# In-projection order: the chunk of latent keys and values ahead of the two chunks of rotary queries and keys

## The chip, the cores and the metric

The kernel runs on one core of one Trainium2 chip. A core has five engines that each work through their own list of instructions in order: PE (TensorE, matrix products), DVE (VectorE), ACT (ScalarE), POOL (GpSimd) and SP (SyncE, which here issues the DMAs). [...] The metric is the device time of one launch in microseconds (us). The median of three runs of the kernel before is 3787.1 us (3786.85 to 3792.39).

## The reference

Two layers of a transformer-like trunk are applied to 128 context tokens and 1024 latent tokens, 1152 tokens of width 1024 in all. One layer begins with one product, the in-projection, whose columns are split into the inputs of three mixers:

```python
z = jnp.einsum('bsd,dn->bsn', h, P['w_in'][l])
hq, hff, hfb, hi, hg, mq, mkv, mkr, gq, gk, gv = jnp.split(z, IN_OFFSETS, axis=-1)
hg_out, s_f, s_b = _hgrn_mixer(hq, hff, hfb, hi, hg, lb, s0f, s0b, P['hg_norm'][l])
ckv = _rms(mkv, P['mla_kv_norm'][l])
gq = _rms(gq.reshape(...), P['gqa_q_norm'][l]);  gk = _rms(gk.reshape(...), P['gqa_k_norm'][l])
gq = _rope_2d(gq, row, col);  ak = concat([gk_c, _rope_2d(gk, row, col)])
```

The HGRN mixer is a gated linear recurrence over the tokens in both directions. The MLA mixer is attention over compressed keys and values (mq, mkv, mkr). The GQA mixer is attention with six query heads and two key heads, normalised per head and rotated in two dimensions (gq, gk, gv). The three outputs go through an output projection and a layer norm, then a SwiGLU feed-forward block and a second layer norm follow.

## The kernel before

The tokens are nine tiles of 128. A layer is four phases: the in-projection with the HGRN recurrence (phase_b), both attentions (phase_c), the output projection (phase_d) and the feed-forward block (phase_e). Products are made exact by splitting each operand into a high and a low part and adding three products (mm3, lines 110 to 112).

In phase_b a *chunk* of the in-projection is 256 columns (288 for chunk "b") for all nine tiles: token_chunk (L355) loads the chunk's weights, and for each tile runs 24 matmuls into a PSUM bank and then evacuates it. The evacuations differ, and they matter here:

- chunk 3 (output gate of HGRN), ev_raw: one ACT copy, one store to DRAM.
- chunks 5 and 6 (rotary queries and keys; called q0 and q1 below), ev_q (L403): ACT squares and copies, DVE sums (L412), POOL forms the reciprocal root in two instructions (L118, L119), DVE scales by it (L415) and by the norm's row (L417, once per tile for q0, twice for q1), POOL rotates (L397 twice, L400, L401), and the tile is stored to the DRAM tensor zq.
- chunk "b" (latent keys and values, values of GQA, rotary part of the MLA key), ev_k (L437): ACT squares and copies, the same two POOL instructions on one column, one DVE instruction (L445), and the rotation on 32 columns only; stored to zk.
- chunk 7 (MLA queries, called mq below), ev_m (L427): ACT squares, the two POOL instructions on one column, one DVE instruction (L434), which frees the PSUM bank.

Beside each tile of mq goes one *turn* of the GQA heads (gqa_turn, L517): it reads zq of one token tile back from DRAM (tile tx), transposes it on PE (L534), copies on ACT (L537, L541), and takes low parts on POOL (L542 and a L104). It needs both q0 and q1 of that tile in DRAM. hgrn_gate (L717) takes the gate chunk through a sigmoid and two POOL products (L726, L728). The first attention group of phase_c needs all ten turns.

hgrn (L572) walks the nine tiles with seven levels and a diagonal each. A level is: DVE forms differences (L641, L644 twice), ACT takes the exponential (L646), POOL makes two products (L648, L650), PE multiplies (L655), DVE writes under a mask (L660). The last L650 of a layer is the last POOL instruction of the recurrence.

The program is not run in the order in which it is written. A list scheduler replays the recorded instructions and writes a fixed order for each engine, in which the matmuls of the chunks that are written behind hgrn fill the gaps of the recurrence on PE. What was written earlier has precedence. The chunks' PSUM banks are few: two ("a") in layer 0, three ("aad") in layer 1 (L341), and the staging tiles st number three (L368). So PE can run only a few tiles ahead of the evacuations.

Of the kernel before, what the change touches and what calls it, by code (L numbers as in the profile page):

```python
# [53 lines left out]
class Build:  # L54
# [280 lines left out]
    def phase_b(self, l, first=None):  # L335
# [4 lines left out]
        b = "b"  # L340
# [14 lines left out]
        def token_chunk(name, evac):  # L355
            ws = self.w_in(*name)
            n = 288 if name[1] == "b" else 256
            for t in range(NT):
                ps = self.ps("A")
                terms = [(self.hts(t, k, 0), self.hts(t, k, 1), hi[:, k - k0, :], lo[:, k - k0, :])  # L360
                         for k0, k1, hi, lo in ws for k in range(k0, k1)]
                self.mm3(ps[:, :n], terms)
                evac(t, ps)
                if t % 2:
                    self.fill()

        def stage():
            return self.t("b2", [P, 384], tag="st", bufs=3)  # L368

        def ev_raw(name):  # L370
            def ev(t, ps):
                st = stage()
                nc.scalar.copy(st[:, :256], ps[:, :256])
                nc.sync.dma_start(z[name][t], st[:, :256])
            return ev
# [7 lines left out]
        def tables(t):  # L383
            tb = self.t("b2", [P, 192], tag="tb", bufs=2)
            nc.sync.dma_start(tb, A["rope_tok"][:, t - 1, :])
            return tb

        def rope(x, tb, off, heads, half):

            w = 4 * half  # L390
            xv = x.rearrange("p (h a s f) -> p h a s f", h=heads, a=2, s=2)
            cos = tb[:, off:off + w].unsqueeze(1).broadcast_to([P, heads, w])
            sin = tb[:, off + w:off + 2 * w].rearrange("p (a s f) -> p a s f", a=2, s=2)
            t2 = self.tmp()
            tv = t2[:, :heads * w].rearrange("p (h a s f) -> p h a s f", h=heads, a=2, s=2)
            for s in range(2):
                nc.gpsimd.tensor_tensor(tv[:, :, :, s, :], xv[:, :, :, 1 - s, :],  # L397
                                        sin[:, :, s, :].unsqueeze(1).broadcast_to([P, heads, 2, half]), op=ALU.mult)
            xm = x.rearrange("p (h w) -> p h w", h=heads)
            nc.gpsimd.tensor_tensor(xm, xm, cos, op=ALU.mult)  # L400
            nc.gpsimd.tensor_tensor(x, x, t2[:, :heads * w], op=ALU.add)  # L401

        def ev_q(half):  # L403
            def ev(t, ps):
                st = stage()
                x = st[:, :256]
                sq = self.tmp()
                nc.scalar.activation(sq[:, :256], ps[:, :256], AF.Square)
                nc.scalar.copy(x, ps[:, :256])
                ss = self.t("small", [P, 4], tag="ss4", bufs=3)  # L410
                r = self.t("small", [P, 4], tag="r4", bufs=3)
                nc.vector.reduce_sum(ss, sq[:, :256].rearrange("p (h f) -> p h f", h=4), axis=AX.X)  # L412
                self.rsq(r, ss, 1 / 64, 4)
                xv = x.rearrange("p (h f) -> p h f", h=4)
                nc.vector.tensor_tensor(xv, xv, r.unsqueeze(2).broadcast_to([P, 4, 64]), op=ALU.mult)  # L415
                for h0, n, g in (((0, 4, 0),) if half == 0 else ((0, 2, 0), (2, 2, 64))):
                    nc.vector.tensor_tensor(xv[:, h0:h0 + n], xv[:, h0:h0 + n],  # L417
                                            rows[:, g:g + 64].unsqueeze(1).broadcast_to([P, n, 64]), op=ALU.mult)
                if t == 0:
                    if half:  # L420
                        nc.sync.dma_start(A["o_gk"][0, l].rearrange("s h f -> s (h f)"), x[:, 128:256])
                else:
                    rope(x, tables(t), 0, 4, 16)
                nc.sync.dma_start(z["q"][t][:, half * 256:half * 256 + 256], x)
            return ev
# [62 lines left out]
        self.hgrn(l, cst, masks)  # L488

        token_chunk((l, 3), ev_raw("g"))  # L490
        token_chunk((l, 5), ev_q(0))
        token_chunk((l, 6), ev_q(1))

# [8 lines left out]
                self.gqa_turn(l, 1, 1, "G")  # L502
            self.gqa_turn(l, 1, t + (t > 0), "G")

        token_chunk((l, "b"), ev_k)
        token_chunk((l, 7), ev_mq)
        self.hgrn_gate(l)
        self.fill(100)
# [920 lines left out]
```

## Time and profile before

| | |
|---|---|
| median of three runs | 3787.1 us |
| profiled execution | 3788.79 us |
| its span, first to last instruction | 3787.0 us |
| mean granted TensorE clock | 0.981 of full |
| PE busy | 3667.2 us (97% of the span) |
| DVE busy | 2021.7 us (53%) |
| ACT busy | 1380.3 us (36%) |
| POOL busy | 1100.7 us (29%) |
| recurrence with chunks b, q0, q1, mq, layer 0 | about 178 to 492 us |
| the same, layer 1 | about 2080 to 2347 us |

A busy PE is no proof of a full PE, since its matmuls are pipelined and their ends are modelled. The granted clock (PEclk) says more: it falls where PE had waited. POOL and DVE, at 29% and 53% of the whole span, are close to full in the two stretches of the recurrence, which are about 15% of the time.

### The profile page before, as it was taken

Reading aid. Unit: us, or ns where it says so; the run is one execution under the profiler, and the core shown is the slowest. Engines: PE = TensorE matmul, PEld = TensorE weight load, DVE = VectorE, ACT = ScalarE, POOL = GpSimd, SP = SyncE. Lnnn points to the kernel's source line nnn. Section 1 sums busy time; section 2 is a strip of 40 time slices with the busy share of each in tenths; the row PEclk is TensorE's granted clock in tenths of the full one; section 3 lists DMA queues with packets and bytes.
Section 4 is the critical chain, followed back from the end, with each engine's and each line's share of the span. In section 5 each row is a group of like instructions: output and inputs, shape, how many; then the busy total and the mean of one; then the engine's idle time right before and its main releaser. Section 6 shows DMA issues by size and latency. Waiting matters only on the chain.

```text
span 3787.0 us, 60397 instructions
## 1 busy us (share of the span) xinstructions
PE 3667.2 (97%) x23734; PEld 3210.9 (85%) x23734; DVE 2021.7 (53%) x3906; ACT 1380.3 (36%) x3283; POOL 1100.7 (29%) x1394
## 2 busy tenths in 40 slices
PE   8999899999999999999999989999999999999997
PEld 6878777788788888999989878778877999999996
DVE  3489456556564333333366894665567533333336
ACT  3433466666341111111144335666654211111111
POOL 1158850211161000000432786511126600000054
PEclk9998899999999999999999998999999999999998
DMA  6521421001134331111231115100012311111131
GB/s 240 179 64 43 117 65 25 15 7 35 59 130 157 101 106 51 51 40 48 96 128 59 51 44 140 28 20 15 7 55 73 114 41 47 41 40 45 45 95 73
DMA packets 185967, 263.78 MB, mean 70 GB/s; under 512 B 68657, under 2 KB 114353, under 8 KB 185170
## 3 DMA queue, kind: packets, MB, share of 16 engines
q1 hardware_dynamic: 185682, 259.92, 21.7%
q8 instruction: 187, 3.06, 0.3%
q14 instruction: 98, 0.80, 0.1%
HBM read 218.47 MB, written 38.77 MB: 68 GB/s over the span
## 4 chain that ended last, share of the span: by engine, by line
PE 81%; DVE 7%; POOL 4%; ACT 3%; issue 2%; DMA 2%; SPq 0%; POOLq 0%; DVEq 0%; ACTq 0%
PE b L110 10%; PE b L112 10%; PE b L111 10%; PE d L855 7%; PE c L806 5%; PE a L110 5%; PE b L784 5%; PE a L111 4%; PE a L112 4%; PE a L784 3%; PE b L655 2%; PE c L110 2%; PE c L112 2%; PE c L111 2%; PE d L111 2%
## 5 line engine op out<-in xcount | busy, mean ns | idle before, releaser
L111 PE MATMUL b<-h,w 128*128 128x384 f32 x1848 | 622.4, 337 | 3.6 <-DVE h L104 2.7
L110 PE MATMUL b<-h,w 128*128 128x384 f32 x1848 | 623.8, 338 | 0.1
L112 PE MATMUL b<-h,w 128*128 128x384 f32 x1848 | 621.8, 337 | 0.0
L103 ACT CAST w<-raw 128x1024 fp32r<-128x1024 f32 (+2 forms) x192 | 198.7, 1036 | 803.4 <-PE c L111 262.7
L104 DVE TENSOR_TENSOR w<-raw,w 128x1024 fp32r<-128x1024 f32 (+3 forms) x188 | 242.1, 1295 | 367.9 <-ACT w L103 362.4
L110 PEld LDWEIGHTS b<-h,w 128*128 128x128 f32 x1848 | 347.4, 188 | 17.8 <-issue 7.6
L111 PEld LDWEIGHTS b<-h,w 128*128 128x128 f32 x1848 | 347.6, 188 | 10.3 <-DVE h L104 4.5
L112 PEld LDWEIGHTS b<-h,w 128*128 128x128 f32 x1848 | 347.5, 188 | 8.0 <-issue 5.0
L1245 POOL TENSOR_TENSOR acc<-acc,lg 128x512 f32<-128x512 f32 x36 | 49.1, 1378 | 935.4 <-DVE acc L1231 931.7
L110 PE MATMUL a<-w,h 128*128 128x256 f32 (+1 forms) x960 | 287.2, 299 | 8.4 <-DVE st L445 4.9
L855 PE MATMUL d<-pt,v 128*64 128x128 f32 x3456 | 288.9, 285 | 0.4 <-DVE m L856 0.4
L111 PE MATMUL a<-w,h 128*128 128x256 f32 (+1 forms) x960 | 281.0, 293 | 0.0
L112 PE MATMUL a<-w,h 128*128 128x256 f32 (+1 forms) x960 | 279.7, 292 | 0.0
L806 PE MATMUL c<-ident,p 128*128 128x128 f32 x1728 | 272.0, 279 | 6.7 <-ACT p L790 2.9
L855 PEld LDWEIGHTS d<-pt,v 128*64 128x64 f32 x3456 | 186.3, 136 | 76.7 <-issue 61.7
L785 DVE TENSOR_REDUCE m<-b 128x1 f32<-128x384 f32 x346 | 188.5, 554 | 112.8 <-PE b L784 112.1
L806 PEld LDWEIGHTS c<-ident,p 128*128 128x128 f32 x1728 | 200.4, 141 | 47.2 <-issue 16.3
L790 ACT ACTIVATE p<-b,nm 128x384 f32<-128x384 f32 x346 | 198.6, 582 | 72.4 <-DVE nm L788 66.3
L110 PEld LDWEIGHTS a<-w,h 128*128 128x128 f32 x960 | 188.1, 196 | 30.9 <-ACT m L380 6.7
L111 PEld LDWEIGHTS a<-w,h 128*128 128x128 f32 x960 | 188.1, 196 | 5.4 <-issue 1.9
L112 PEld LDWEIGHTS a<-w,h 128*128 128x128 f32 x960 | 187.5, 195 | 4.2 <-issue 1.7
L1202 DVE TENSOR_TENSOR gate<-gate,b 128x384 f32<-128x384 f32 x110 | 60.9, 553 | 242.5 <-PE b L112 242.5
(391 smaller groups left out, 8483.1 us busy)
## 6 DMA issues: line engine op xcount, KB each, us to landing
w<-in_w_ada_dram SPq DMA_DIRECT2D x96, 512.0 KB, 4.4
raw<-in_w_ffn_in_dram SPq DMA_DIRECT2D x88, 512.0 KB, 3.5
raw<-in_w_ffn_out_dram SPq DMA_DIRECT2D x44, 512.0 KB, 3.6
raw<-in_w_in_a_dram SPq DMA_DIRECT2D x32, 512.0 KB, 4.4
xs<-acc SPq DMA_DIRECT2D x36, 256.0 KB, 4.1
u<-xs SPq DMA_DIRECT2D x36, 256.0 KB, 2.5
raw<-in_w_out_dram SPq DMA_DIRECT2D x16, 512.0 KB, 4.3
tx<-zq SPq DMA_DIRECT2D x72, 96.0 KB, 2.4
```

Of the source, the lines that this page charges most:

```text
L103: self.nc.scalar.copy(hi, src)
L104: (eng or self.nc.vector).tensor_tensor(lo, src, hi.bitcast(F32), op=ALU.subtract)
L110: self.nc.tensor.matmul(out, ah, bh, start=i == 0, stop=False)
L111: self.nc.tensor.matmul(out, ah, bl, start=False, stop=False)
L112: self.nc.tensor.matmul(out, al, bh, start=False, stop=i == n - 1)
L655: nc.tensor.matmul(ps[:, j * P:(j + 1) * P], X[r, j, :], Q[r, j, :], start=True, stop=True)
L784: nc.tensor.matmul(ps, a, bfn(c * 384, 384), start=k == 0, stop=k == len(ops) - 1)
L785: nc.vector.reduce_max(mx[:, c:c + 1], ps, axis=AX.X)
L790: nc.scalar.activation(pt[:, c * 384:(c + 1) * 384], tiles[c], AF.Exp, bias=nm, accum_out=sm[:, u, c:c + 1])
L806: nc.tensor.transpose(pt[:, (2 * i + u) * P:(2 * i + u + 1) * P], g["p"][u][:, kt * P:(kt + 1) * P], self.ident)
L855: nc.tensor.matmul(po[h * 64:(h + 1) * 64, :P], g["v"](k, h), turned[s // 2][:, o:o + P], start=k == 0, stop=k == 8)
L1202: nc.vector.tensor_tensor(g, g, ps[:, :384], op=ALU.mult)
```

## The change

One line of phase_b moves: chunk "b" is written in front of q0 and q1 instead of behind them. Nothing else is edited.

```diff
@@ phase_b
         self.hgrn(l, cst, masks)
 
         token_chunk((l, 3), ev_raw("g"))
+        token_chunk((l, "b"), ev_k)
         token_chunk((l, 5), ev_q(0))
         token_chunk((l, 6), ev_q(1))
 
...
-        token_chunk((l, "b"), ev_k)
         token_chunk((l, 7), ev_mq)
```

The same instructions are issued, with the same operands and sizes. Their order in the engines' lists changes in the stretch from the first of these chunks to the first attention group, in both layers; the rest of the lists is the same but for a few neighbours exchanged.

On PE in layer 0, the two rows behind the last products of the recurrence (L682, L679). Before, they and six more tiles are chunk b (128x288):

```order
L682 MATMUL c_3370<-it_3136,at_3140 128x64 x2
L679 MATMUL c_3370<-Sf_1658,m_466 128x128
L682 MATMUL c_3370<-it_3136,at_3140 128x64 x2
L110 MATMUL a_4652<-w_4554,h_71_245 128x288
L111 MATMUL a_4652<-w_4555,h_71_245 128x288
```

In the changed kernel, at the same place:

```order
L682 MATMUL c_3370<-it_3136,at_3140 128x64 x2
L679 MATMUL c_3370<-Sf_1658,m_466 128x128
L682 MATMUL c_3370<-it_3136,at_3140 128x64 x2
L110 MATMUL a_4808<-w_4528,h_74_250 128x256
L111 MATMUL a_4808<-w_4529,h_74_250 128x256
```

Behind the recurrence stand now three tiles of q1 and nine of mq in place of seven of b and nine of mq.

On POOL in layer 0, the rows from the last L650 on. Before (rsv, r with x1: reciprocal roots of b; st 128x32: rotation of b; it: the HGRN gate):

```order
L650 TENSOR_TENSOR Q_3353<-qT_3138,E_3348 128x256
L400 TENSOR_TENSOR st_4524<-st_4524,tb_4537 128x256
L119 TENSOR_TENSOR r_960_4598<-rsv_961_4601,mhalf_76 128x1
L119 TENSOR_TENSOR r_966_4637<-rsv_967_4640,mhalf_76 128x1
L400 TENSOR_TENSOR st_4634<-st_4634,tb_4644 128x32
L726 TENSOR_TENSOR it_5431<-it_5431,u_5433 128x256
L401 TENSOR_TENSOR st_4524<-st_4524,t_4539 128x256
L401 TENSOR_TENSOR st_4634<-st_4634,t_4646 128x32
```

In the changed kernel (rsv, r with x4 and st 128x256: q1):

```order
L650 TENSOR_TENSOR Q_3353<-qT_3138,E_3348 128x256
L728 TENSOR_TENSOR it_5431<-it_5431,hgn_464 128x256
L118 TENSOR_SCALAR rsv_979_4702<-ss_977_4699 128x4
L400 TENSOR_TENSOR st_4649<-st_4649,tb_4662 128x256
L119 TENSOR_TENSOR r_978_4700<-rsv_979_4702,mhalf_76 128x4
L401 TENSOR_TENSOR st_4649<-st_4649,t_4664 128x256
L397 TENSOR_TENSOR t_4710<-st_4695,tb_4708 128x8x16 x2
L400 TENSOR_TENSOR st_4695<-st_4695,tb_4708 128x256
```

Seven tiles of q1 are rotated behind the last L650 now; before, it was the end of one.

On POOL in layer 1 of the changed kernel, the rows up to the first reciprocal root of mq (r_4619; te: a turn's copy, t_23459: rotation of the last q1 tile):

```order
L104 TENSOR_TENSOR K_4608_23471<-te_23837,K_4607_23470 128x128
L726 TENSOR_TENSOR it_23985<-it_23985,u_23987 128x256
L397 TENSOR_TENSOR t_23459<-st_23444,tb_23457 128x8x16 x2
L118 TENSOR_SCALAR rsv_4620_23514<-ss_4618_23511 128x1
L118 TENSOR_SCALAR rsv_4632_23573<-ss_4630_23570 128x1
L118 TENSOR_SCALAR rsv_4641_23623<-ss_4639_23620 128x1
L726 TENSOR_TENSOR it_23992<-it_23992,u_23994 128x256
L728 TENSOR_TENSOR it_23985<-it_23985,hgn_19173 128x256
L400 TENSOR_TENSOR st_23444<-st_23444,tb_23457 128x256
L119 TENSOR_TENSOR r_4619_23512<-rsv_4620_23514,mhalf_76 128x1
```

All nine rotations of q1 but the last instruction of the last one, seven turns, and seven and six of the gate's two products stand ahead of it; before, the first reciprocal root of mq stood behind chunk b's small instructions and ahead of all turns.

## Rows read from the trace of the kernel before

**Rows 1.** Windows, both recurrences and tails: length; busy PE, PEld, DVE, ACT, POOL; clock.

```profile
245.00:417.00 172.00, 155.80 (x1081) 136.23 (x1081) 155.94 (x360) 66.77 (x148) 147.42 (x199) 0.89 0.15 44
417.00:492.00 75.00, 63.09 (x455) 60.94 (x451) 16.76 (x37) 28.47 (x87) 46.07 (x101) 0.91 0.54 148
2105.00:2298.00 193.00, 180.34 (x1258) 158.62 (x1256) 164.47 (x397) 76.01 (x175) 164.03 (x238) 0.91 0.17 52
2298.00:2347.00 49.00, 42.73 (x343) 40.83 (x339) 15.36 (x30) 24.10 (x69) 38.23 (x72) 0.95 0.71 193
```

**Rows 2.** Windows of 20 us: before q0 begins, and in layer 0's tail.

```profile
220.00:240.00 20.00, 20.00 (x141) 16.01 (x139) 15.53 (x37) 7.50 (x15) 7.55 (x9) 1.00 0.26 80
440.00:460.00 20.00, 15.10 (x103) 14.31 (x102) 4.81 (x8) 11.41 (x32) 18.50 (x40) 0.87 0.78 202
```

**Rows 3.** Groups by line, DVE, 245 to 417 us: busy, mean ns, idle before.

```profile
L415 DVE TENSOR_TENSOR st<-st,r 128x256 f32<-128x256 f32 x18 | 13.4, 742 | 3.6 <-POOL r L119 3.6
L417 DVE TENSOR_TENSOR st<-st,rows 128x128 f32<-128x128 f32 x18 | 7.9, 470 | 0.1
L412 DVE TENSOR_REDUCE ss<-t 128x4 f32<-128x256 f32 x18 | 7.4, 409 | 0.3
```

**Rows 4.** Groups by line, DVE, 417 to 492 us.

```profile
L434 DVE SCALAR_TENSOR_TENSOR st<-a,r,rows 128x256 f32<-128x256 f32 x9 | 4.3, 483 | 16.9 <-POOL r L119 16.9
L445 DVE SCALAR_TENSOR_TENSOR st<-a,r,rows 128x128 f32<-128x128 f32 x9 | 3.1, 350 | 26.4 <-POOL r L119 20.6 <-DMA tx<-zq 5.8
```

**Rows 5.** Groups by line, POOL, 245 to 417 us.

```profile
L119 POOL TENSOR_TENSOR r<-rsv,mhalf 128x4 f32<-128x4 f32 x18 | 19.8, 1104 | 0.3
L397 POOL TENSOR_TENSOR t<-st,tb 128x128 f32<-128x128 f32 x32 | 16.0, 516 | 6.1 <-DVE st L417 5.3 <-ACT kT L614 0.8
L401 POOL TENSOR_TENSOR st<-st,t 128x256 f32<-128x256 f32 x15 | 12.8, 850 | 0.2
L118 POOL TENSOR_SCALAR rsv<-ss 128x4 f32<-128x4 f32 x18 | 5.0, 275 | 9.4 <-DVE ss L412 8.5
```

**Rows 6.** Groups by line, POOL, 417 to 492 us.

```profile
L542 POOL TENSOR_TENSOR Q<-te,Q 64x384 fp32r<-64x384 f32 x9 | 9.9, 1102 | 0.7
L119 POOL TENSOR_TENSOR r<-rsv,mhalf 128x1 f32<-128x1 f32 x18 | 9.9, 550 | 0.7
L728 POOL TENSOR_TENSOR it<-it,hgn 128x256 f32<-128x256 f32 x8 | 5.9, 734 | 0.2
L104 POOL TENSOR_TENSOR K<-te,K 128x128 fp32r<-128x128 f32 x10 | 5.3, 530 | 0.7
L118 POOL TENSOR_SCALAR rsv<-ss 128x1 f32<-128x1 f32 x16 | 3.2, 198 | 19.5 <-ACT t L432 13.3 <-ACT t L442 5.4
L401 POOL TENSOR_TENSOR st<-st,t 128x256 f32<-128x256 f32 x1 | 0.7, 727 | 0.0
```

**Rows 7.** Timeline of POOL: start, duration; last L650 and mq's roots, both layers.

```profile
415.66 0.72 POOL L650 TENSOR_TENSOR Q<-qT,E 128x256 f32<-128x256 f32 x1
...
477.82 0.55 POOL L119 TENSOR_TENSOR r<-rsv,mhalf 128x1 f32<-128x1 f32 x1
...
490.61 0.55 POOL L119 TENSOR_TENSOR r<-rsv,mhalf 128x1 f32<-128x1 f32 x1
...
2296.45 0.74 POOL L650 TENSOR_TENSOR Q<-qT,E 128x256 f32<-128x256 f32 x1
...
2344.45 0.55 POOL L119 TENSOR_TENSOR r<-rsv,mhalf 128x1 f32<-128x1 f32 x1
```

**Rows 8.** Timeline of PE: two neighbouring matmuls of an mq tile.

```profile
475.07 0.28 PE L111 MATMUL a<-w,h 128*128 128x256 f32 x1
475.19 0.28 PE L112 MATMUL a<-w,h 128*128 128x256 f32 x1
```

**Rows 9.** Chain of waits by line, 245 to 417 us.

```profile
by line: PE b L655 14.1%; issue 10.6%; DVE E L644 6.8%; PE a L110 6.5%; PE a L111 5.6%; POOL Q L650 5.4%; PE a L112 5.3%; DVE at L660 5.1%; POOL X L648 4.2%; POOL r L119 3.8%; DVE E L641 3.4%; PE c L682 2.4%; DVE st L415 2.3%; DVE st L417 2
```

**Rows 10.** Waits of PE, 417 to 492 us: total, times, longest.

```profile
PE a L110 <- DVE st L434: 2.9, 2, 1.7
```

## The prediction

> **What bounds the kernel now.** I read the windows of the two recurrences first, then the groups by line of POOL and DVE in them, then the timeline of POOL behind them, and the waits of PE last. "Recurrence" is the stretch up to POOL's last L650 of a layer; "tail" is what follows, up to POOL's reciprocal root for the last tile of mq, after which the first attention group can take its banks.
>
> In the recurrences DVE is busy 155.9 of 172 us (91%) and 164.5 of 193 (85%), POOL 147.4 (86%) and 164.0 (85%) [rows 1]. PE is busier by its own count, but its clock averages 0.89 and 0.91 there, so it did wait. The chain of waits passes through PE, DVE and POOL in turn and none holds it alone [rows 9]. The first part is another matter: at 220 to 240 us, before q0, PE is busy 20.00 of 20.00 at full clock [rows 2]. So the recurrence is filled by PE at its beginning, and held by DVE and POOL where q0 and q1 are evacuated.
>
> The tails differ by layer. From the end of the last L650 (415.66 + 0.72 = 416.4) to the end of mq's last root (490.61 + 0.55 = 491.2) layer 0 takes 74.8 us; layer 1 takes from 2297.2 to 2345.0, 47.8 us [rows 7]. POOL has room there: 46.1 busy of 75 and 38.2 of 49; DVE has much (16.8 and 15.4) [rows 1].
>
> **The change part by part.** No instruction is added or removed. Work moves over the last L650.
>
> 1. *Recurrence, DVE.* I count in the order what DVE has done up to its last L641. Layer 0: L412 18 before and 12 now, L415 18 and 11, L417 27 and 13 (all of the missing ones are q1's halves), L445 none and 9. In times [rows 3, 4]: 6 x 0.409 + 7 x 0.742 + 14 x 0.470 - 9 x 0.350 = 11.1 us less. Layer 1: 5, 6 and 12 fewer, 6 more L445: 2.0 + 4.5 + 5.6 - 2.1 = 10.0 us less. If DVE alone set the pace, the last L650 would come 11 and 10 us earlier. If PE did, it would come no earlier. PE gets no relief: in layer 0 seven tiles of b come into the recurrence and three of q1 leave it. A matmul of 256 columns takes 0.12 us [rows 8], so a tile of 24 takes 2.8; with 288 columns I estimate 3.2 from that. 7 x 3.2 - 3 x 2.8 = 14 us more for PE, and PE's unfilled time by its own count is 172 - 155.8 = 16.2 us [rows 1], so it just fits; later than now is excluded only by that margin. The ends are -11 and 0, and the rows speak for one end early in the recurrence and for the other later, so I take the middle: **-5.5 us in layer 0, -5 in layer 1**.
>
> 2. *Tail, POOL.* This is what is late next. POOL works in order, and the roots of mq now stand behind the rotations of q1, seven turns and most of the gate. I sum what stands from the last L650 to mq's first root, with it, durations from [rows 5, 6] (L400 is taken as L401, L726 as L728, both of one shape):
> layer 0: 13 L400 and L401 x 0.727 = 9.5; 12 L397 x 0.516 = 6.2; 6 L119 of four columns x 1.104 = 6.6; 6 L118 x 0.275 = 1.7; 15 gate products x 0.734 = 11.0; 7 L542 x 1.102 = 7.7; 8 L104 x 0.530 = 4.2; L118 and L119 of mq 0.9; sum 47.8 us.
> Layer 1: 12 x 0.727, 12 x 0.516, 5 x 1.104, 5 x 0.275, 13 x 0.734, 7 x 1.102, 8 x 0.530 and 1.1: sum 44.4 us.
> To this comes POOL's own idle time. At none it is 0; at the 14% of the recurrence [rows 1] it is 7 us; at the 7.5% of the nearest stretch, 440 to 460 us [rows 2], 3.5. SP's queue pulls upward, since each turn's read of zq waits in it for the store of the rotation before; the other way, the means for L397 and L119 were taken beside a busy DVE. I take **2 us**.
>
> A PSUM bank of mq is free only after its root and L434, and PE has waited for L434 already [rows 10]. With two banks in layer 0, mq's third tile starts 0.5 us (L434, [rows 4]) after the first root; with three in layer 1, the fourth does. From then mq goes tile by tile at the spacing of the roots now, (490.61 - 477.82) / 4 = 3.2 us [rows 7]; the last root ends 1.4 us after its matmuls (ACT's square, L118 and L119).
> Layer 0: 47.8 + 2 + 0.5 + 7 x 3.2 + 1.4 = 74.1 us against 74.8: **-0.7**.
> Layer 1: 44.4 + 2 + 0.5 + 6 x 3.2 + 1.4 = 67.5 us against 47.8: **+19.7**.
> The layers part because layer 1's tail is short today: six of b's tiles are evacuated before its last L650, only two are in layer 0, and a third bank lets PE run through.
>
> [...] L401 of this shape takes 0.850 us in the recurrence and 0.727 behind it, where DVE rests [rows 5, 6]. [...]
>
> 3. *The rest.* Weight loads and splits of b come earlier and those of q0 and q1 later, as many as before, beside the recurrence; if that cover went, one DVE split of a chunk's weights would stand in front of a level, under 2 us. The stores to zk are read only in phase_c and come earlier. Evacuations of b are lighter than those they replace. Phases c, d and e keep their orders, so what the tails win or lose goes through whole.
>
> Sum: -5.5 - 0.7 = -6.2 in layer 0, -5 + 19.7 = +14.7 in layer 1, together **+8.5 us**. The profiled execution lasted 3788.8 us with a span of 3787.0; the median of the runs is 3787.1, 1.7 less, and 8.5 is added to that: **3795.6 us**, 0.2% slower.
>
> **The rivals.**
>
> *A, the forecast.* POOL's backlog of q1 behind the last L650 holds mq in layer 1 for longer than both recurrences gain. 3796 us, 3787 to 3805 with the bounds of its terms.
>
> *B, the recurrence gains from both queues (faster).* The evacuation of b is light on DVE and on POOL. The chain goes through both, level by level [rows 9], and POOL loses about as much as DVE: per layer some 24 us of q's instructions go out (layer 0: 6 x 1.379 + 12 x 0.516 + 12 x 0.83 = 24.4 [rows 5]) and b's smaller ones come in, about half of that. If half of the net relief of 12 adds to DVE's 11, the recurrences end 17 us earlier each: 3787 + 19 - 34 = 3772 us. For it: DVE and POOL at 85 to 91%. Against it: PE full at 220 to 240 us without any q in the way, and the 14 us more for PE in layer 0. It decides from 13.3 us per layer on (19 - 26.6 is 0.2% faster).
>
> *C, the two cancel.* Only DVE sets the pace: -11 and -10, then -0.7 + 19.7: -2 us, 3785. That the change does nothing would end here too, but the order shows that it moves q1 and mq as described.
>
> [...]
>
> **How the numbers follow.** A 0.38, D 0.12, C 0.25, B 0.25. About 0.2%, 7.6 us, is what a measurement of this kernel can tell from no change. Of A 0.30 lies beyond it and 0.08 within; D is slower, C within, B faster. Slower 0.42, same 0.33, faster 0.25. The range of 3772 to 3814 reaches from B's price to D's. A alone has 3787 to 3805.
>
> **What would show it.** In the profile after, layer 0's last L650 should come at about 411 us instead of 415.7 and layer 1's 10 to 12 us earlier against its own start of the recurrence, if the first term is right; POOL should then be busy over 90% for 45 us behind each, with PE's clock low and PE's waits put down to L434 or L534; mq's first root should be about 50 and 46 us behind the last L650, and the tail of layer 1 about 67 us. The forecast is wrong if the recurrences end over 13 us earlier, or if PE runs mq in layer 1 without waiting for POOL, so that its tail stays under 55 us.

## The result and the profile after

The changed kernel takes 3812.4 us (median of 4 runs, 3806.0 to 3816.0), the kernel before 3788.2 (4 runs): a ratio of 1.0055, interval 1.0042 to 1.0068. By the medians that is 24 us slower; by the ratio it is 21, with an interval of 16 to 26. It lies inside the stated range and on the side forecast, but is almost three times the 8.5 us of the sum. The profiled execution took 3805.96 us, the lowest of its runs, with a span of 3804.2, 17.2 us over that of before; so the traces hold 17 of the 24 us.

Four moments of each layer, in us of the profiled executions (the start of a layer's first L650, the end of its last L650, the end of mq's last root, and the first product of the attention with the values, L855; some products of scores, L784, begin earlier):

| | layer 0 before | after | layer 1 before | after |
|---|---|---|---|---|
| recurrence, first to last L650 | 242.1 | 242.4 | 238.0 | 232.8 |
| tail, to mq's last root | 74.8 | 78.6 | 47.8 | 66.7 |
| last L650 to first attention product | 82.7 | 86.2 | 59.2 | 77.7 |
| first L650 to first attention product | 324.8 | 328.6 | 297.1 | 310.5 |

The last line gives +3.8 and +13.4 us, the whole of the span's difference.

Windows of the changed kernel that answer to [rows 1], with their ends moved to its own last L650 and last root (columns: length; busy PE, PEld, DVE, ACT, POOL; clock):

```profile
245.00:415.00 170.00, 157.59 (x1142) 137.49 (x1141) 145.32 (x343) 68.65 (x159) 138.50 (x208) 0.96 0.18 53
415.00:494.00 79.00, 55.42 (x375) 52.53 (x374) 22.00 (x49) 28.30 (x76) 54.82 (x91) 0.83 0.44 123
2105.00:2301.00 196.00, 185.63 (x1324) 162.35 (x1324) 162.09 (x393) 76.57 (x180) 154.78 (x231) 0.95 0.18 55
2301.00:2365.00 64.00, 44.22 (x307) 39.92 (x306) 20.11 (x40) 24.86 (x67) 48.14 (x81) 0.84 0.54 147
```

The recurrences are fuller on PE than before (clock 0.96 and 0.95 for 0.89 and 0.91) and lighter on DVE and POOL. The tails are emptier: the clock is 0.83 and 0.84 where it was 0.91 and 0.95.

POOL's timeline at the rows that answer to [rows 7] (start, duration): the last L650, mq's first root (run together with its neighbours, x2 and x3) and its last, in both layers:

```profile
414.47 0.72 POOL L650 TENSOR_TENSOR Q<-qT,E 128x256 f32<-128x256 f32 x1
...
466.62 1.07 POOL L119 TENSOR_TENSOR r<-rsv,mhalf 128x1 f32<-128x1 f32 x2
...
493.25 0.55 POOL L119 TENSOR_TENSOR r<-rsv,mhalf 128x1 f32<-128x1 f32 x1
...
2295.20 0.90 POOL L650 TENSOR_TENSOR Q<-qT,E 128x256 f32<-128x256 f32 x1
...
2341.65 1.60 POOL L119 TENSOR_TENSOR r<-rsv,mhalf 128x1 f32<-128x1 f32 x3
...
2362.30 0.55 POOL L119 TENSOR_TENSOR r<-rsv,mhalf 128x1 f32<-128x1 f32 x1
```

The first root ends 52.0 and 46.1 us behind the last L650. What PE does meanwhile in layer 1, in windows of 4 us:

```profile
2328.00:2332.00 4.00, 2.25 (x16) 1.99 (x15) 0.00 (x0) 1.16 (x3) 3.60 (x7) 0.90 0.16 49
2332.00:2336.00 4.00, 0.69 (x1) 0.29 (x1) 1.77 (x3) 1.09 (x5) 3.84 (x6) 0.52 0.19 60
2336.00:2340.00 4.00, 0.00 (x0) 0.00 (x0) 0.89 (x2) 1.31 (x5) 3.60 (x9) 0.50 0.38 103
2340.00:2344.00 4.00, 2.31 (x9) 1.93 (x10) 0.97 (x2) 1.30 (x3) 4.00 (x8) 0.50 0.28 78
2344.00:2348.00 4.00, 4.00 (x30) 4.00 (x28) 0.48 (x1) 0.89 (x3) 3.65 (x6) 0.77 0.54 183
2348.00:2352.00 4.00, 4.00 (x37) 4.00 (x36) 0.95 (x2) 0.47 (x2) 1.37 (x4) 1.00 0.69 164
```

PE does almost nothing for 8 us (0.69 us busy) while POOL is busy over 90%; then it works on without a gap, first at a granted clock of 0.50. PE's waits in the two tails (415 to 494 us, then 2297 to 2365; total, times, longest) are these. The last row is the longest of before in layer 0's tail, which stands beside the one of [rows 10]:

```profile
PE a L110 <- ACT st L409: 10.8, 3, 8.0
PE c L534 <- DMA tx<-zq: 7.4, 2, 5.8
```

```profile
PE c L534 <- DMA tx<-zq: 8.9, 3, 7.1
PE b L784 <- POOL K L104: 5.0, 3, 2.9
PE a L110 <- ACT st L409: 2.5, 3, 1.2
PE a L110 <- DVE st L434: 0.8, 1, 0.8
```

```profile
PE a L110 <- DVE st L445: 4.9, 2, 4.1
```

The wait named is hardly L434, the bank of mq. It is the copy of a q1 tile out of its bank (L409, which needs a staging tile), and the reading back of zq for a turn, which stands in PE's list ahead of an mq tile. Both come from the same place: q1 is still on its way through ACT, DVE, POOL and DRAM. The 5.0 us before L784 are products of scores that wait for the turns' low parts on POOL.

### The profile page after: what moved, and what is told of

It reads as the page before. It is cut to its first block, busy times and chain, and to the rows that moved or that the text cites. A ratio compares the mean times of both kernels' runs of the same rounds, so it can differ in the third digit from the quotient of the medians.

```text
span 3804.2 us, 60406 instructions
## 1 busy us (share of the span) xinstructions
PE 3665.6 (96%) x23734; PEld 3206.1 (84%) x23734; DVE 2012.2 (53%) x3906; ACT 1378.5 (36%) x3283; POOL 1100.0 (29%) x1394
## 4 chain that ended last, share of the span: by engine, by line
PE 76%; DVE 5%; POOL 3%; ACT 3%; issue 2%; DMA 1%; SPq 0%; POOLq 0%; DVEq 0%; ACTq 0%
PE b L110 10%; PE b L112 10%; PE b L111 10%; PE d L855 7%; PE c L806 5%; PE b L784 4%; PE a L110 4%; PE a L112 3%; PE a L111 3%; PE a L784 3%; PE c L110 2%; PE c L112 2%; PE c L111 2%; PE d L110 2%; PE d L111 2%
## 5 line engine op out<-in xcount | busy, mean ns | idle before, releaser
L104 DVE TENSOR_TENSOR w<-raw,w 128x1024 fp32r<-128x1024 f32 (+2 forms) x188 | 238.3, 1274 | 365.9 <-ACT w L103 353.4
L110 PEld LDWEIGHTS b<-h,w 128*128 128x128 f32 x1848 | 347.7, 188 | 17.8 <-issue 7.6
L855 PE MATMUL d<-pt,v 128*64 128x128 f32 x3456 | 289.4, 285 | 0.4 <-DVE m L856 0.4
L855 PEld LDWEIGHTS d<-pt,v 128*64 128x64 f32 x3456 | 186.6, 136 | 76.6 <-issue 61.5
```

The costliest lines, as they stand in the source:

```text
L104: (eng or self.nc.vector).tensor_tensor(lo, src, hi.bitcast(F32), op=ALU.subtract)
L110: self.nc.tensor.matmul(out, ah, bh, start=i == 0, stop=False)
L855: nc.tensor.matmul(po[h * 64:(h + 1) * 64, :P], g["v"](k, h), turned[s // 2][:, o:o + P], start=k == 0, stop=k == 8)
```

## The experiments

All are timed beside the kernel before, whose medians were 3789.4 us (for the first four), 3788.7 (the _dve pair, after_norot and before_nomul), 3789.8 (st4) and 3786.1 (before_norot). The names: l0_only and l1_only make the change in one layer; the ending _dve moves work from POOL to DVE; norot and nomul leave work out; st4 has a fourth staging tile. Except for st4, whose lists stay the same on all engines but SP, each of these kernels gets new lists from the scheduler, so its neighbours' order changes along with the work that is moved.

**One layer at a time.** The chunk b is written in front only if l is 0 (l0_only) or only if l is 1 (l1_only):

```diff
         token_chunk((l, 3), ev_raw("g"))
+        if l == 0:
+            token_chunk((l, "b"), ev_k)
...
-        token_chunk((l, "b"), ev_k)
+        if l != 0:
+            token_chunk((l, "b"), ev_k)
```

> Chunk b goes in front of q0 and q1 in layer 0 only; layer 1 keeps the order of before. Theory A (POOL's backlog of q1 holds mq in the tail; layer 0's tail was long before, so it loses little there): +2 to +6 us against before, about 3792. Rival R1 (the price lies in b's early place itself, alike in both layers): half of the change's 24 us, about +12, 3800.

> Chunk b goes in front in layer 1 only. Theory A: nearly the whole price, +14 to +20 us, about 3805, with the last L650 to the last mq root at about 67 us in layer 1 as in the changed kernel. Rival R1 (alike in both layers): about +12, 3800.

Measured: 3796.1 us for layer 0 alone, ratio 1.0019 (1.0010 to 1.0028), +6.7 us; 3805.5 for layer 1 alone, 1.0042 (1.0030 to 1.0055), +16.1. The two add to 22.8 of the 24 us, and the stretch from the first L650 to L855 in the layer that has the change is the one of the changed kernel (327.9 for 328.6 us, 310.5 for 310.5), so the terms can be judged apart: the sum had -6.2 for layer 0 and +14.7 for layer 1. Layer 1 is right; layer 0 has the wrong sign and is 13 us off by the medians. Rival R1, +12 in each layer, falls; theory A's +2 to +6 for layer 0 is missed by little. One profile is a coarse scale: in l0_only's, the same stretch of layer 1, which keeps the order of before, takes 303.3 us for 297.1.

**Other places for b.** b between q0 and q1 (mid: 3, q0, b, q1, mq), and q0 and q1 first (q_first: q0, q1, 3, b, mq):

```diff
         token_chunk((l, 3), ev_raw("g"))
         token_chunk((l, 5), ev_q(0))
+        token_chunk((l, "b"), ev_k)
         token_chunk((l, 6), ev_q(1))
...
-        token_chunk((l, "b"), ev_k)
```

```diff
-        token_chunk((l, 3), ev_raw("g"))
         token_chunk((l, 5), ev_q(0))
         token_chunk((l, 6), ev_q(1))
+        token_chunk((l, 3), ev_raw("g"))
```

> Chunk b stands between q0 and q1 in both layers. In the order, q1's rotations behind the last L650 are eight in layer 0 (52 us of POOL work up to mq's first root) but only two to three in layer 1 (9.5 us). Theory A: layer 0 pays about as in the changed kernel (+2 to +8), layer 1 nothing (tail about 48 us, not 67): 3790 to 3796. Rival R1 (b's place ahead of rotary work costs by itself): half the change or more in each layer, +12 or more, 3800 and above.

> A version meant to beat both: q0 and q1 go in front of the HGRN gate chunk, which is followed by b and mq, in both layers. Theory A with its other side (light evacuations belong last, heavy ones into the part of the recurrence in which POOL has room: 7.6 of 20 us busy at 220 to 240 us): no rotation is left behind the last L650, tails no longer than before, and the recurrences shorter by 2 to 8 us each: 3772 to 3784. Rival (PE is full in that part, so nothing is gained early, and the gate's chain, now later, waits in the tail): 3788 or up to 10 us slower.

Measured: mid 3797.2, ratio 1.0022 (1.0013 to 1.0031); q_first 3793.0, 1.0008 (0.9999 to 1.0017). mid's time lies between the bounds of both theories, but its layers tell them apart: in layer 0, with eight rotations of q1 behind the last L650, the tail is 80.9 us (74.8 before), in layer 1, with two, it is 40.2 (47.8 before), where R1 wanted a price in both. Its recurrences are longer, 245.1 and 243.5 us. q_first did not gain, as its rival had it: its tails are shorter (63.0 and 46.8 us) and its recurrences longer (251.4 and 246.0). Work that one of these orders takes out of the tail it has in the recurrence.

**What DVE is worth in the recurrence.** The kernel before without the products by the norm's row of q0 and q1:

```diff
-                for h0, n, g in (((0, 4, 0),) if half == 0 else ((0, 2, 0), (2, 2, 64))):
-                    nc.vector.tensor_tensor(xv[:, h0:h0 + n], xv[:, h0:h0 + n],
...
```

> The kernel before without the products by the norm's row of q0 and q1 (L417, 27 instructions and 12.7 us of DVE per layer; so its output differs). It tells what paces the recurrence where q0 and q1 are evacuated. If DVE does (first term of the forecast at its full end), the recurrences of 242.1 and 238.0 us shorten by 10 to 13 us each: 3763 to 3769 us. If PE does in layer 0, its recurrence stays within 3 us of 242 and only layer 1's falls, by 5 to 12: 3776 to 3785 us. If neither moves, another engine or the order sets the pace: 3785 to 3792 us.

Measured: 3765.1 us, ratio 0.9942 (0.9929 to 0.9954), -23.6: the time of the full end of DVE's term, but not for its reason, since the recurrences did not become shorter: 245.9 and 241.8 us. The windows of [rows 1] in this kernel:

```profile
245.00:417.00 172.00, 157.79 (x1134) 138.41 (x1132) 145.61 (x333) 67.19 (x153) 150.85 (x213) 0.92 0.16 49
417.00:492.00 75.00, 65.11 (x484) 58.73 (x483) 24.28 (x57) 39.89 (x117) 46.83 (x94) 0.95 0.57 158
2105.00:2298.00 193.00, 183.90 (x1349) 163.94 (x1348) 151.52 (x351) 75.11 (x185) 164.81 (x256) 0.95 0.21 63
```

DVE has 10 and 13 us less to do in the same stretch, and PE runs 53 and 91 instructions more in it. The gain shows behind it: the tails fall from 74.8 to 54.7 us and from 47.8 to 31.5; from the first L650 to L855 the layers are 16.6 and 6.9 us shorter. So here relief of DVE, in the order that the scheduler then wrote, bought matmuls of the chunks that are done before the last L650, and not an earlier last L650.

**POOL relieved in the tail.** In both orders, the turns' low parts and the gate's products go to DVE in phase_b:

```diff
-            nc.gpsimd.tensor_tensor(dq[64:128], pq[64:128], dq[64:128].bitcast(F32), op=ALU.subtract)
-        self.split(K[0][:, slot], K[1][:, slot], y[:, 3 * P:], eng=nc.gpsimd)
+            (nc.vector if g == 1 else nc.gpsimd).tensor_tensor(dq[64:128], pq[64:128], dq[64:128].bitcast(F32), op=ALU.subtract)
+        self.split(K[0][:, slot], K[1][:, slot], y[:, 3 * P:], eng=nc.vector if g == 1 else nc.gpsimd)
...
-            nc.gpsimd.tensor_tensor(g, g, sg, op=ALU.mult)
+            nc.vector.tensor_tensor(g, g, sg, op=ALU.mult)
...
-            nc.gpsimd.tensor_tensor(gv, gv, self.hgn.unsqueeze(1).broadcast_to([P, 4, 64]), op=ALU.mult)
+            nc.vector.tensor_tensor(gv, gv, self.hgn.unsqueeze(1).broadcast_to([P, 4, 64]), op=ALU.mult)
```

> The changed kernel with the turns' low parts (L542 and a L104) and the gate's two products (L726, L728) on DVE instead of POOL, in phase_b of both layers; nothing is left out. By the order POOL then has 25.7 and 23.1 us of work from the last L650 to mq's first root instead of 47.8 and 44.5. Theory A (POOL's work in order ahead of mq's roots sets the tails): both tails shorten by about 20 us (layer 1 from 66.8 to about 46, layer 0 from 78.6 to about 57), and the time is 3765 to 3780 us, below the kernel before. Rival R (the round trip of zq through SP and DRAM and the three staging tiles set the tails, POOL's share is cover): both tails lose less than 6 us each, 3800 us or more. Between: DVE takes the place of POOL in the recurrence, which then grows by some us per layer, 3780 to 3800.

> The kernel before with the same instructions moved to DVE; nothing is left out. Theory A: layer 1's tail of 47.8 us runs at a clock of 0.95 already and loses 0 to 5 us, layer 0's of 74.8 has 7 tiles of b and 9 of mq for PE (about 48 us) and loses 10 to 20: 3765 to 3780 us, so that the order of chunks makes less than 8 us of difference once POOL is relieved. Rival R: no tail moves by over 5 us, 3780 to 3790 us, and the change still costs 20 us on top of it. If DVE in the recurrence suffers from the gate's products, the time is 3790 us or more.

Measured: after_dve 3789.6 us, ratio 1.0005 (0.9996 to 1.0013); before_dve 3775.7, 0.9970 (0.9958 to 0.9982), the lowest time of a kernel that leaves nothing out. In after_dve the tails fall to 62.5 and 61.3 us, by 16.1 in layer 0 and 5.4 in layer 1, and the recurrences stay within 1.6 us: theory A's 20 us are nearly met in layer 0, rival R's "less than 6" in layer 1, and the time lies between the two. In before_dve the tails are 60.9 and 44.0 us, as theory A had them. POOL's work in the tail therefore costs time in both orders, 23 us by the medians (19 by the ratios) in the changed one and 13 (11) in the other. But the order still costs 13.9 us with POOL relieved, where theory A had less than 8. POOL in layer 1 of after_dve, last L650, first and last root of mq:

```profile
2282.41 0.73 POOL L650 TENSOR_TENSOR Q<-qT,E 128x256 f32<-128x256 f32 x1
...
2321.78 1.07 POOL L119 TENSOR_TENSOR r<-rsv,mhalf 128x1 f32<-128x1 f32 x2
...
2343.86 0.55 POOL L119 TENSOR_TENSOR r<-rsv,mhalf 128x1 f32<-128x1 f32 x1
```

POOL has 21 us less to do ahead of the first root, which comes only 6.9 us earlier (39.2 us behind the last L650 for 46.1); up to it POOL is now busy 23.5 of 39 us:

```profile
2283.00:2322.00 39.00, 26.51 (x175) 23.51 (x175) 22.66 (x62) 18.83 (x50) 23.47 (x38) 0.90 0.56 150
```

No engine is full there. PE still waits for zq, with the L682 that ends the recurrence behind it:

```profile
PE c L534 <- DMA tx<-zq: 4.9, 2, 4.5
PE c L682 <- DVE at L660: 2.7, 2, 2.3
```

So a full POOL was the first limit in layer 1's tail, and a second one stood close behind it.

**Is the second limit the staging ring?** A fourth staging tile, in the changed kernel and in both kernels with _dve:

```diff
-            return self.t("b2", [P, 384], tag="st", bufs=3)
+            return self.t("b2", [P, 384], tag="st", bufs=4)
```

> The changed kernel with four staging tiles st instead of three; the engines' lists of instructions stay the same but for SP's, where two or three DMAs change places. In layer 1's tail of the change PE waited for L409 (a staging tile) and stood still from 2332 to 2342 us with POOL busy over 90%. Theory P (POOL's work in order ahead of mq's roots is what ends last): the fourth tile only lets q1 run further ahead of POOL, the tails stay within 3 us of 78.6 and 66.8 and the time is 3806 to 3814 us. Theory S (the three staging tiles, each held from ACT's copy through POOL's rotation to the end of its store, pace q1): both tails shorten by 5 to 10 us, 3792 to 3803 us.

> The changed kernel with turns and gate on DVE (3789.6 us, tails of about 63.8 and 61.8 us) and four staging tiles as well. There q1's tiles were copied at 2286.5, 2295.2, 2300.5, 2305.9 and 2312.2 us, about 5.5 us apart, with PE needing 2.9 and POOL about 4 each. Theory S (with POOL relieved the three staging tiles are next): 3 to 4 us apart, layer 1's tail down to 50 to 55 us, time 3772 to 3782 us. Theory P (what is left is PE's own work, 264 matmuls of chunks and the turns, and the way of the last zq through DRAM): the tails stay within 3 us, 3784 to 3791 us.

> The kernel before with turns and gate on DVE (3775.7 us) and four staging tiles. If staging also held q0, q1 and b in the recurrences of this order, 3764 to 3773 us, the lowest time of all that leave nothing out; if DVE, POOL and the order set its pace, 3773 to 3779 us.

Measured: after_st4 3808.4, ratio 1.0056 (1.0043 to 1.0068); after_dve_st4 3785.7, 0.9991 (0.9982 to 1.0000); before_dve_st4 3776.6, 0.9969 (0.9957 to 0.9982). In after_st4 layer 0's tail is 78.3 us (78.6 without the tile), and layer 1's does not get shorter; there the first and the last root end 46.2 and 68.1 us behind the last L650 (46.1 and 66.7 without it):

```profile
2297.79 0.90 POOL L650 TENSOR_TENSOR Q<-qT,E 128x256 f32<-128x256 f32 x1
...
2344.31 1.61 POOL L119 TENSOR_TENSOR r<-rsv,mhalf 128x1 f32<-128x1 f32 x3
...
2366.22 0.55 POOL L119 TENSOR_TENSOR r<-rsv,mhalf 128x1 f32<-128x1 f32 x1
```

Theory S falls for the changed kernel: the wait for L409 was a wait for an earlier tile of q1 to get through, and a place more to wait in does not hasten that. With POOL relieved the fourth tile shortens layer 1's tail by 2.9 us (61.3 to 58.4; layer 0's is 63.2 for 62.5) and the median by 3.9, and gives the order of before nothing. The cost of the order is then 9.1 us (3785.7 - 3776.6) instead of 13.9. The intervals of after_dve and after_dve_st4 overlap a little, so it is likely and not certain that the ring holds some 4 of the 14 us; it does not hold most of them.

**q1's rotation taken out.** Both orders without the rotation of q1's eight tiles of latent tokens:

```diff
-                else:
+                elif half == 0:
                     rope(x, tables(t), 0, 4, 16)
```

> The changed kernel without the rotation of q1 (L397 twice, L400, L401 for its eight tiles of latent tokens; so its output differs). From the last L650 to mq's first root POOL has 12.6 and 4.7 us left instead of 47.8 and 44.5; the chain of q1 to zq is also 2.5 us shorter per tile. Theory A: tails shorten to what PE and the turns need, layer 1 from 66.8 to about 45, layer 0 from 78.6 to about 55, and the recurrences by 0 to 5 us: 3760 to 3775 us. Rival R (round trip of zq): the tails follow the stores of q1, which still wait for their turn on PE, DVE and the staging ring: layer 1 stays over 58 us, 3790 us or more. If this kernel gains much and the one with the products on DVE does not, it is the production of q1 and its round trip, not POOL's place in front of mq.

> The kernel before without the rotation of q1 (L397 twice, L400, L401 of eight tiles; so its output differs); the changed kernel without it took 3762.8 us. It tells whether the order of the chunks still costs anything when q1 leaves POOL with its root alone. If q1's rotations on POOL and the way of its last tiles through them are what the change pays for, its cost of 24 us falls below 8 and this kernel takes 3755 to 3767 us. If what is paid for is something else (PE's work left behind the recurrence, the turns, SP's queue), the cost stays at 14 us (as with turns and gate on DVE) or more, and this kernel takes 3749 us or less.

Measured: after_norot 3762.8 us, ratio 0.9935 (0.9922 to 0.9947); before_norot 3765.9, 0.9945 (0.9931 to 0.9958), both as the theory that q1's rotations are what is paid for had them. The order costs nothing any more: the difference is -0.10% of 3788 us, -4 us, and the ends of the intervals (0.9947 against 0.9931) leave +6 at most. The rows of layer 1, first of after_norot, then of before_norot, where the last root ends 34.7 us behind the last L650:

```profile
2276.53 1.45 POOL L650 TENSOR_TENSOR Q<-qT,E 128x256 f32<-128x256 f32 x1
...
2284.72 0.55 POOL L119 TENSOR_TENSOR r<-rsv,mhalf 128x1 f32<-128x1 f32 x1
...
2318.20 0.54 POOL L119 TENSOR_TENSOR r<-rsv,mhalf 128x1 f32<-128x1 f32 x1
```

```profile
2277.26 0.73 POOL L650 TENSOR_TENSOR Q<-qT,E 128x256 f32<-128x256 f32 x1
...
2312.11 0.55 POOL L119 TENSOR_TENSOR r<-rsv,mhalf 128x1 f32<-128x1 f32 x1
```

after_norot's first root ends 7.3 us behind the last L650 instead of 46.1, and its tail is 40.8 us instead of 66.7. That is still 6.1 us longer than before_norot's, but L855 follows its last root after 8.8 us and not 16.8; from the first L650 to L855 the changed order takes 1.6 us more in layer 0 and 3.8 less in layer 1. What the change pays for is q1's way through POOL behind the last L650, on which both mq's roots and the turns' zq depend. Without the rotation POOL's work and q1's way both get shorter, so this does not say how the 24 us divide between the two; the _dve pair says that: about 10 go with the turns and the gate off POOL (24.2 - 13.9; by the ratios 8), about 14 remain.

## Why the prediction was right, and where it was off

*Step 1, the recurrence.* Wrong in form, and in layer 0 by its whole size: the term of -5.5 measured +0.3 (242.1 to 242.4), and the last L650 began at 414.5 us where about 411 was announced. The relief of DVE itself was there: 145.3 us busy of 170 for 155.9 of 172. What came in its place was PE's work done early. The order had listed it (the tiles of b and q1 left behind the recurrence), and the sum had it only as 14 us that PE must fit into the recurrence, not as work that is gone from the tail: in layer 0's recurrence the trace has 757 matmuls of chunks instead of 674, 83 x 0.12 = 10 us. That this is near the 11.1 worked out from DVE is not shown to be more than chance. In the kernel without the norm's products such work shortened the tail; here the tail was held by q1 on POOL, so it was lost in PE's waits. In layer 1 the recurrence measured -5.2 for -5, with only 12 matmuls of chunks more (759 for 747); the 10 to 12 us that the prediction announced there as a sign fitted neither its own term nor the trace. The size isn't settled: l1_only has 232.9 us too, after_st4, whose lists are the same on all engines but SP, 237.8; and with the order of before it was 238.0 and, in l0_only, 242.0. One profile differs from the next by 4 to 5 us here, as much as the term. The sign is likely real, for the changed order is the shorter in each pair of kernels that differ in the order alone: 234.4 for 239.1 us with _dve, 234.7 for 239.3 with _dve and st4, 237.9 for 240.0 with norot. In layer 0 the same pairs give +0.8, -0.6 and +4.3.

*Step 2, layer 1's tail.* Right: +18.9 for +19.7; first root 46.1 us behind the last L650 for 46.4; last root 66.7 for 67.5. In the 46 us from 2296 to 2342 POOL was busy 41.4, so its work was 3 us less than summed and its idle time 2.6 us more, and PE ran mq afterwards at 2.8 us a tile instead of 3.2. The mechanism was one of two: two ends fell together. PE came to the matmuls of mq's fourth tile at 2342.8, after 7.1 us for zq that ended at 2340.9 and 0.8 for L434. I had set only the bank against POOL.

*Step 2, layer 0's tail.* -0.7 measured +3.8. First root 52.0 us behind the last L650 for 49.8: from 415 to 467 us POOL was busy 45.2 of 52, 2.6 less than summed, and idle 6.8, the upper bound and not the 2 taken. Then 26.6 us to the last root for 24.3. PE's timeline in the changed kernel shows the largest single piece of it: the turn that waited for zq, and mq's third tile behind it:

```profile
467.13 1.09 PE L534 MATMUL c<-ident,tx 128*128 128x128 f32 x4 [5.77 <-DMA tx<-zq]
467.87 0.56 PE L110 MATMUL a<-w,h 128*128 128x256 f32 x1
468.23 0.41 PE L111 MATMUL a<-w,h 128*128 128x256 f32 x1
468.44 0.41 PE L112 MATMUL a<-w,h 128*128 128x256 f32 x1
```

The matmuls follow each other at 0.21 us, at a granted clock of 0.50 (468 to 470 us), where [rows 8] had 0.12. From 472.0 us on they follow at 0.12 again, and the tile's 24 take 4.7 us instead of 2.8.

*The sum.* By the traces: +0.3 and +3.8 in layer 0 against -6.2, -5.2 and +18.9 in layer 1 against +14.7; 17.8 against 8.5, nearly all of the miss in layer 0. The 6.4 us from the profiled execution to the median lie outside the trace; layer 1's recurrence, which varied by 5 us between profiles of one order, could hold most of them, and that isn't shown.

*The rivals.* B and C needed recurrences that end 10 to 17 us earlier; layer 0's did not move, and layer 1's by 5 us at most. D, the price of a lower clock in the tail, is the range's upper end, 3814 us; no run shows that price. What the traces show in its place: the clock did fall in both tails (0.83 and 0.84 for 0.91 and 0.95), but behind the first root one mq tile of each layer was slow, 4.7 and 4.3 us instead of 2.8, and the time came from PE standing still. So the mechanism of A was right, and the size was luck: 3812 us lies outside A's own 3787 to 3805, and the stated range holds it only because it reached up to D's price.

*What stays open.* With POOL at 60%, q1's last tiles still take 39 us behind the last L650 in layer 1. The staging ring is not most of it; what sets their pace among ACT, DVE, POOL, DRAM and the turns between them in PE's list was not separated.

## What to carry to other kernels

An order of chunks is a choice of what is still under way when the long serial part ends. Put the chunk with the longest way from its matmuls to its last reader (here q1: four engines, DRAM and back, then PE again) early enough that this way runs beside the serial part, and leave chunks there whose bank is free after one or two instructions. That has an end: q_first, which put q0 and q1 first of all, gained nothing. Where one engine is relieved inside a scheduled serial part, ask what becomes of the time: in the kernel without the norm's products, and in layer 0 of the change, it bought more filler work of PE and not an earlier end, and it was worth something only as long as the filler was what the next part waited for.

## What was not expected of the hardware

The subtraction L542 took 1102 ns in the mean on POOL [rows 6], with eight of the nine at 1.0 us, and 605 ns on DVE, in layer 1's tail of after_dve:

```profile
L542 DVE TENSOR_TENSOR Q<-te,Q 64x384 fp32r<-64x384 f32 x8 | 4.8, 605 | 2.2 <-ACT Q L541 1.9
L415 DVE TENSOR_TENSOR st<-st,r 128x256 f32<-128x256 f32 x6 | 2.5, 420 | 2.4 <-POOL r L119 2.4
```

L415, with both inputs in SBUF, took 420 ns there beside a POOL busy 60%. In the same stretch of the changed kernel, beside a POOL busy 90%, it took twice that:

```profile
L415 DVE TENSOR_TENSOR st<-st,r 128x256 f32<-128x256 f32 x5 | 4.2, 843 | 16.7 <-POOL r L119 16.7
```

The busy share is not what decides: in layer 0's tail of the changed kernel, beside a POOL busy 87%, six L415 took 597 ns in the mean. The single ones, 11 in both tails, take either 0.42 to 0.43 us or 0.94 to 0.96. The six long ones all began 0.05 to 0.07 us behind a POOL instruction of 0.71 to 0.73 us (L401 or L728) with two inputs in SBUF; the five short ones met none at their start. Where POOL's L542 began 0.04 or 0.05 us behind L415, as in three of these five, L415 kept its time and L542 took 1.23 us instead of 1.0. One case of the second kind and one of the first, in layer 1 (start, duration):

```profile
2321.70 0.43 DVE L415 TENSOR_TENSOR st<-st,r 128x256 f32<-128x256 f32 x1 [6.59 <-POOL r L119]
2321.74 1.23 POOL L542 TENSOR_TENSOR Q<-te,Q 64x384 fp32r<-64x384 f32 x1
...
2334.68 0.72 POOL L401 TENSOR_TENSOR st<-st,t 128x256 f32<-128x256 f32 x1
2334.75 0.94 DVE L415 TENSOR_TENSOR st<-st,r 128x256 f32<-128x256 f32 x1 [0.35 <-POOL r L119]
```

In these rows the one that begins first keeps its time (L415 0.43 us, L401 0.72), and the other takes longer: L542 1.23 us instead of 1.0, L415 0.94 instead of 0.43. Why is not shown. The prediction's sum had the rotations in the tail at the 0.727 us that L401 took behind the recurrence [rows 6]. That held for L401 (0.72 to 0.73 us in both tails of the changed kernel), while DVE's L415 kept its 0.42 to 0.43 us there in five cases of eleven.
